# A decoder layer on one core: causal pooling by transposes and doubled sums in three groups, and a decay in two factors

## The chip, the core and the metric

The kernel runs on one core of a Trainium2 chip. The metric is the device time of one execution in microseconds. Before the change it is 1568.56 us, the median of 3 runs (1568.49 to 1571.36). The names used below: TensorE (PE) multiplies matrices, VectorE (DVE) and ScalarE (ACT) work element by element, GpSimd is POOL, and SP issues most of the transfers.

## The reference

One layer of a decoder on 256 tokens of 2048 channels, all in float32:

```
h = rmsnorm(x)
q, k, v, z, b, a, p, g_a, g_b = split(h @ w_in)
q, k, v = silu(causal_conv4(q, k, v));  q, k = l2norm(q), l2norm(k)
o   = gated_delta_rule(q, k, v, decay(a), sigmoid(b))   # 16 heads of 128, chunks of 64
y_a = rmsnorm(o) * silu(z)
y_b = (trailing_mean(p) - p) @ pool_w * pool_scale       # 4 groups of 512 channels
x  += (sigmoid(g_a) * y_a + sigmoid(g_b) * y_b) @ w_out
h = rmsnorm(x);  gate, up = split(h @ w_up)              # 2 x 5632
x  += (gelu(causal_conv3(gate)) * up) @ w_down
out = rmsnorm(x)
```

The trailing mean runs over the last 2, 4, 8 or 16 tokens, one window for each group of 512 channels; at the start of the sequence it divides by the tokens that there are. The delta rule is a recurrence over the tokens with a decay for each token and head: what token i gives to token j is weighted by the exponential of the sum of the log-decays between them.

## The kernel before

**Weights.** Nearly all of the work is products with weights. A weight matrix comes in tiles of 256 rows by 512 columns, 512 KB each, loaded over SP's queue (`load`, L124). ACT casts a tile to the matmul's format (L143, `whi`), and DVE subtracts that from the tile to get the part that the cast lost (L151, `wlo`). The input is split in the same way, and three matmuls (L181, L182, L183) give high times high, low times high and high times low. So `gemm_a` makes 12 matmuls of a weight tile. Four raw tiles and three pairs of split tiles are held, and `weights()` begins the tile two ahead of the one that it hands out (`AHEAD = 2`). The products of the MLP are made in the same way (L205 and L206, L1044 to L1046).

**Groups.** The mixing half runs over 4 groups, `g`, of 4 heads and 512 channels. In each, the products with weights come in the order K, Q, V, P (the pooled input), GB (the gate of the pooled branch), the pool product (the pooled input with `pool_w`, two tiles only, `nk = 4`), Z and GA. All but the pool product have 8 tiles. Between the matmuls runs the side work:

- Functions in the list `later` are run when the next product comes to its second tile. The convolutions of K and Q (`conv_silu`), the pooling (`pooled`) and the turning of the mixed result (`mixed`) come in this way.
- `side()` is called after every 6 matmuls. It takes one step of the generator `gdn`, the delta rule of the current group; a `yield` there is such a step, half a weight tile.

**Pooling.** `pooled` (L880 to L891) turns the evicted input `ev` and pools it in one go. It multiplies `ev` with a band matrix in float32 (L885, L887): the band holds one over the window, in the first tokens one over the count, less the identity, all times one half. The bands of the four windows are built once, by `fixed_parts` (L529 on), with memset, copies, `affine_select` and subtractions. ACT casts the result to `phi` (L890), and DVE subtracts to get `plo` (L891). The pool product reads both. The turning elsewhere is done by `turned`: 8 transposes (L226) into two PSUM tiles, `psg`, of which there are four buffers in all.

**The delta rule, `gdn`.** The 256 tokens lie in two halves of 128. Its steps, in order:

1. *Decay.* For two heads at a time DVE makes the triangular tiles r (L647, L648). Matmuls (L655, L656) sum the log-decays within each half, `pd0` and `pd1`; another (L658, with `onesr`, a tile of ones) sums those of the second half up to each of its tokens, `pdx`. ACT takes the exponentials (L659, L660), and for the pair of halves those of `pdx` with the first half's remaining sum, `tail`, as bias (L663). POOL clears the upper triangles (L665).
2. *Grams.* Matmuls of keys with keys and queries (L674, L676). DVE multiplies them with the norm factors and the decay to `ga0` (first half against both halves, L689) and `ga1` (second half, L693).
3. *Transfers.* The diagonal blocks of 32 go through memory, `cdd` (L707) and then `lb` (L710), so that one tile holds all blocks for the solve.
4. *Query norms.* A transpose on DVE, a reduction, the selection matmul (L725), and four small operations, `ro` (L729).
5. *Solve.* `LATE[g]` steps later, `tb` is set to the identity (L737), and 31 pairs of operations, `tmp` (L740) and `tb` (L742), three pairs a step, invert the blocks of 32. `tb` goes through memory (`tbd`, L747, then `TT`, L750) and is turned on DVE to `T` (L761).
6. *Merges.* Small matmuls join the blocks of 32 to 64 (from L782) and the blocks of 64 to 128 (to L811).
7. *Outputs.* `w1` (L817) solves the first half, `pr` (L822) carries it into the second, where `vt` takes it off (L823), `w2` (L827) solves the second half; `po[0]` and `po[1]` (L832 to L835) are the outputs of the halves. `po[1]` sums two products in PSUM, one with `ga0[384:512]` and `w1`, one with `ga1` and `w2`. Squares, norms, the gates (`gated`) and the turning follow.

**What sets the order.** The program is written as one stream. A scheduler orders each engine's instructions by its own model of time. Two places are ordered by hand: the start, and for the last group PE alone. There PE keeps the written order from the GA product on (`fixed_order`). In that group the delta rule waits before its merges (`while g == 3 and not ending`) until 6 tiles of GA are done; `step(n)` leaves n steps between the merges instead of one, and the first 6 tiles of two output products (`early`) cover what follows. The buffers of `mtile` (`m0` to `m7`) hold `phi` and `plo` of a group and later its mixed result; the other tiles have tags in the pool `mp`, and a tile with a tag in use waits for the one before it.

Of the kernel before, what the change touches and what calls it, by code (L numbers as in the profile page):

```python
# [13 lines left out]
P = 128  # L14
# [20 lines left out]
def kernel(  # L35
# [32 lines left out]
    def nm(s):  # L68
        cnt[0] += 1
        return f"{s}_{cnt[0]}"  # L70
# [376 lines left out]
    nc.vector.reciprocal(icnt, icnt)  # L447
    nc.vector.tensor_scalar(icnt, icnt, 0.5, None, op0=ALU.mult)
    idh = mp.tile([P, P], F32, name="idh")
# [19 lines left out]
    bat = mp.tile([64, 2, S], F32, tag="u", name="bat")  # L469
    nc.vector.tensor_copy(bat, pba[:64])  # L470
# [58 lines left out]
    def fixed_parts():  # L529
        for g, win in enumerate(WINDOWS):  # L530
            bd = bands[:, g, :]
            nc.gpsimd.memset(bd, 0.5 / win)
            nc.vector.tensor_copy(bd[:, 0:PAD], icnt[:, g, :])
            for cs in (slice(0, P + PAD), slice(P + PAD, NB)):
                b = bd[:, cs]
                n = cs.stop - cs.start
                nc.gpsimd.affine_select(b, b, pattern=[[1, n]], compare_op=ALU.is_ge, fill=0.0, base=0,
                                        channel_multiplier=-1)
                nc.gpsimd.affine_select(b, b, pattern=[[-1, n]], compare_op=ALU.is_ge, fill=0.0, base=win - 1,
                                        channel_multiplier=1)  # L540
                nc.vector.tensor_tensor(b[:, 0:P], b[:, 0:P], idh, op=ALU.subtract)
        nc.gpsimd.memset(Ta, 0.0)
        nc.gpsimd.memset(TTa, 0.0)
# [85 lines left out]
    def gdn(g, kq, vt, conv, res):  # L629
# [5 lines left out]
        sj = mp.tile([P, 2, 4], F32, tag="sj", name=nm("sj"))  # L635
        dec0 = mp.tile([P, 4, S], F32, tag="dec0", name=nm("dec0"))
        dec1 = mp.tile([P, 4, P], F32, tag="dec1", name=nm("dec1"))
        for hp in range(2):

            h0 = 2 * hp  # L640
            rx = []
            for part, gp in (("h", ghi.bitcast(F32)), ("l", glo)):
                r0 = mp.tile([P, 2, P], F32R, tag="r0" + part, name=nm("r0"))
                r1 = mp.tile([P, 2, P], F32R, tag="r1" + part, name=nm("r1"))
                for i in range(2):
                    hh = 4 * g + h0 + i
                    nc.vector.tensor_scalar(r0[:, i], tri, gp[:, 0, hh : hh + 1], None, op0=ALU.mult)  # L647
                    nc.vector.tensor_scalar(r1[:, i], tri, gp[:, 1, hh : hh + 1], None, op0=ALU.mult)  # L648
                rx.append((r0, r1))
            yield  # L650
            pd0 = pg([P, 2, P])
            pdx = pg([P, 2, P])
            pd1 = pg([P, 2, P])
            for n, (r0, r1) in enumerate(rx):
                mm(pd0, lowr, r0, start=(n == 0), stop=(n == 1))  # L655
                mm(pd1, lowr, r1, start=(n == 0), stop=(n == 1))  # L656
            for n, (r0, r1) in enumerate(rx):
                mm(pdx, onesr, r1, start=(n == 0), stop=(n == 1))  # L658
# [5 lines left out]
            for d in (dec0[:, h0 : h0 + 2, 0:P], dec1[:, h0 : h0 + 2, :]):  # L664
                nc.gpsimd.affine_select(d, d, pattern=[[0, 2], [1, P]], compare_op=ALU.is_ge, fill=0.0, base=0,  # L665
                                        channel_multiplier=-1)
            yield
        for hp in range(2):
# [18 lines left out]
            for h in (h0, h0 + 1):  # L687
                pg0, pg1 = grams[h - h0]
                nc.vector.scalar_tensor_tensor(ga0[:, h, :].rearrange("p (a s) -> p a s", a=2),  # L689
                                               pg0.rearrange("p (a s) -> p a s", a=2), sj[:, 0, h : h + 1],  # L690
                                               dec0[:, h, :].unsqueeze(1).to_broadcast([P, 2, S]),
                                               op0=ALU.mult, op1=ALU.mult)
                nc.vector.scalar_tensor_tensor(ga1[:, h, :].rearrange("p (a s) -> p a s", a=2),  # L693
                                               pg1, sj[:, 1, h : h + 1],
# [70 lines left out]
        while g == 3 and not ending:  # L765
            yield

        def step(n):
# [81 lines left out]
    for g in range(4):  # L850
# [24 lines left out]
        ps = gemm_a(xh, xl, KD)  # L875
        e = evict(ps)
        phi = mtile(g, [P, 4, S], F32R, nm("phi"))
        plo = mtile(4 + g, [P, 4, S], F32R, nm("plo"))

        def pooled(e=e, g=g, phi=phi, plo=plo):  # L880
            for f2 in range(2):
                pt = pg([P, 2, S])
                for ff in range(2):
                    fs = slice((2 * f2 + ff) * P, (2 * f2 + ff + 1) * P)
                    mm(pt[:, ff, P:S], e[:, 1, fs], bands[:, g, P + PAD : NB], start=True, stop=False,  # L885
                       skip_group_check=True)
                    mm(pt[:, ff, 0 : P + PAD], e[:, 0, fs], bands[:, g, 0 : P + PAD], start=False, stop=True,  # L887
                       skip_group_check=True)
                fs = slice(2 * f2, 2 * f2 + 2)
                nc.scalar.copy(phi[:, fs, :], pt)  # L890
                nc.vector.tensor_tensor(plo[:, fs, :], pt, phi[:, fs, :].bitcast(F32), op=ALU.subtract)  # L891

        later.append(pooled)

# [6 lines left out]
        tb = gate(gemm_a(xh, xl, KD), "th")  # L901
        ps = gemm_a(lambda k, t: phi[:, k, t * P : (t + 1) * P], lambda k, t: plo[:, k, t * P : (t + 1) * P], 4)
        yb = mp.tile([P, 2, 512], F32, tag="yb", name=nm("yb"))
# [227 lines left out]
```

## Time and profile before

| | before |
|---|---|
| median of 3 runs | 1568.56 us |
| the profiled execution | 1568.66 us |
| its span in the profile | 1566.9 us |
| mean granted clock of TensorE | 0.999 |
| weight loads issued by SP: w_in, w_up, w_down, w_out | 224, 176, 88, 32 of 512 KB |
| weight loads: pool_w | 8 of 512 KB |
| moved by all transfers | 304.23 MB, 194 GB/s in the mean |

The profile is of one execution. Its page gives the busy time of each engine and its share of the span, the chain of work that ended last, and groups of instructions. A group's line reads: source line, engine, operation, output and inputs, shape, number of instructions, then the busy time, the mean of one in nanoseconds, and the idle time before them with what ended it. A time line gives start and duration in microseconds from the start of the span, then the instruction, and in square brackets how long the engine stood idle before it and for what. A line of the list of waits reads: engine, output and line that waited, an arrow, what it waited for, then the time in all, the number of waits, and the longest. PE records overlap, since matmuls are pipelined: the distance from start to start is what a matmul costs in a row of them.

### The profile page before, as it was taken

To read this page: it belongs to the slowest core of one execution; us is meant where nothing else is said; L and a number is where in the kernel's file an instruction comes from. 1 tells how busy PE (TensorE), PEld (TensorE's weight loads), DVE (VectorE), ACT (ScalarE), POOL (GpSimd) and SP (SyncE) were. 2 spreads that over 40 slices of the span, in tenths; PEclk is the share of its full clock that TensorE was granted. 3 is DMA by queue.
4 is the path that set the end of the run, shared out by engine and by line. 5 is a ranking of instruction groups with operands and counts; after the bars stand their busy time and mean duration, and the time that the engine had idled before them with its cause. 6 is when DMAs were issued, how large, how long until landed. Compare 5 with 4: busy or idle time off the path is not lost.

```text
span 1566.9 us, 21271 instructions
## 1 busy us (share of the span) xinstructions
PE 1555.7 (99%) x8022; PEld 1307.4 (83%) x8022; DVE 1078.9 (69%) x1671; ACT 745.2 (48%) x956; POOL 43.3 (3%) x69
## 2 busy tenths in 40 slices
PE   9999999999999999999999999999999999999997
PEld 8878888888888888787888888888888888888886
DVE  6898749895698758796656666776666667444444
ACT  6545446354554546354544544444444444343443
POOL 2110001000010001000000000000000000000000
PEclk9999999999999999999999999999999999999999
DMA  8676657666676656665655555566556556656662
GB/s 272 199 229 199 195 161 220 196 201 178 181 220 196 198 162 193 212 204 169 216 185 177 189 189 188 188 190 189 188 186 191 189 187 213 199 191 210 202 224 89
DMA packets 168229, 304.23 MB, mean 194 GB/s; under 512 B 19234, under 2 KB 22834, under 8 KB 167998
## 3 DMA queue, kind: packets, MB, share of 16 engines
q1 hardware_dynamic: 165104, 297.84, 61.3%
q10 hardware_dynamic: 3022, 5.03, 0.9%
q8 instruction: 63, 1.03, 0.3%
q14 instruction: 40, 0.33, 0.1%
HBM read 297.56 MB, written 5.27 MB: 193 GB/s over the span
## 4 chain that ended last, share of the span: by engine, by line
PE 98%; DMA 1%; issue 1%; SPq 0%; ACT 0%; DVE 0%; POOLq 0%; POOL 0%
PE psm L183 15%; PE psm L181 15%; PE psm L182 15%; PE psm L205 10%; PE psg L205 10%; PE psg L206 5%; PE psm L206 5%; PE psg L1044 2%; PE psg L1046 2%; PE psg L1045 2%; PE psm L1045 2%; PE psm L1046 2%; PE psm L1044 2%; PE psm L312 1%; PE psg L674 1%; PE psg L226 1%
## 5 line engine op out<-in xcount | busy, mean ns | idle before, releaser
L151 DVE TENSOR_TENSOR wlo<-raw,whi 128x1024 fp32r<-128x1024 f32 x522 | 637.2, 1223 | 391.4 <-ACT whi L143 381.8
L143 ACT CAST whi<-raw 128x1024 fp32r<-128x1024 f32 x524 | 551.2, 1053 | 705.6 <-PE psm L182 313.0
L183 PE MATMUL psm<-wlo,xhl 128*128 128x512 f32 x864 | 339.7, 393 | 0.0
L181 PE MATMUL psm<-whi,xhl 128*128 128x512 f32 x864 | 338.9, 392 | 0.0
L182 PE MATMUL psm<-whi,xhl 128*128 128x512 f32 x864 | 338.5, 392 | 0.0
L205 PE MATMUL psm<-fhl,whi 128*128 128x512 f32 x704 | 246.2, 396 | 0.0
L205 PE MATMUL psg<-fhl,whi 128*128 128x512 f32 x704 | 238.0, 395 | 0.0
L206 PE MATMUL psm<-fhl,wlo 128*128 128x256 f32 x704 | 194.4, 279 | 0.0
L182 PEld LDWEIGHTS psm<-whi,xhl 128*128 128x128 f32 x864 | 162.2, 188 | 33.4
L183 PEld LDWEIGHTS psm<-wlo,xhl 128*128 128x128 f32 x864 | 162.3, 188 | 32.9 <-DVE wlo L151 0.2
L181 PEld LDWEIGHTS psm<-whi,xhl 128*128 128x128 f32 x864 | 162.3, 188 | 32.6
L206 PE MATMUL psg<-fhl,wlo 128*128 128x256 f32 x704 | 178.8, 279 | 0.0
L205 PEld LDWEIGHTS psm<-fhl,whi 128*128 128x128 f32 x704 | 131.4, 188 | 30.5
L205 PEld LDWEIGHTS psg<-fhl,whi 128*128 128x128 f32 x704 | 129.2, 188 | 24.2
L206 PEld LDWEIGHTS psg<-fhl,wlo 128*128 128x128 f32 x704 | 132.5, 188 | 6.9
L206 PEld LDWEIGHTS psm<-fhl,wlo 128*128 128x128 f32 x704 | 132.5, 188 | 1.1
L1044 PE MATMUL psg<-whi,hhi 128*128 128x512 f32 x168 | 65.5, 390 | 0.0
L1045 PE MATMUL psg<-whi,hlo 128*128 128x512 f32 x168 | 65.4, 389 | 0.0
L1044 PE MATMUL psm<-whi,hhi 128*128 128x512 f32 x168 | 65.4, 389 | 0.0
L1046 PE MATMUL psm<-wlo,hhi 128*128 128x512 f32 x168 | 65.4, 389 | 0.0
L1045 PE MATMUL psm<-whi,hlo 128*128 128x512 f32 x168 | 65.4, 389 | 0.0
L1046 PE MATMUL psg<-wlo,hhi 128*128 128x512 f32 x168 | 59.0, 389 | 0.0
(262 smaller groups left out, 1522.5 us busy)
## 6 DMA issues: line engine op xcount, KB each, us to landing
raw<-in_w_in_dram SPq DMA_DIRECT2D x224, 512.0 KB, 4.1
raw<-in_w_up_dram SPq DMA_DIRECT2D x176, 512.0 KB, 4.5
raw<-in_w_down_dram SPq DMA_DIRECT2D x88, 512.0 KB, 4.3
raw<-in_w_out_dram SPq DMA_DIRECT2D x32, 512.0 KB, 3.6
mv<-vrow SPq DMA_DIRECT2D x12, 512.0 KB, 5.6
taps<-in_conv_qkv_w_dram SPq DMA_DIRECT2D x16, 256.0 KB, 5.9
raw<-in_pool_w_dram SPq DMA_DIRECT2D x8, 512.0 KB, 5.9
vrow<-ev SPq DMA_DIRECT2D x4, 512.0 KB, 3.1
```

Of the source, the lines that this page charges most:

```text
L143: nc.scalar.copy(hi, raw)
L151: last_split[0] = nc.vector.tensor_tensor(lo, raw, hi.bitcast(F32), op=ALU.subtract).ins
L181: mm(ps[:, t, :], lh(k, t), hi[:, kk, :], start=(k == 0), stop=False)
L182: mm(ps[:, t, :], ll(k, t), hi[:, kk, :], start=False, stop=False)
L183: mm(ps[:, t, :], lh(k, t), lo[:, kk, :], start=False, stop=(k == nk - 1))
L205: mm(ps[f], hi[:, kk, fs], rhl(k), start=(k == 0), stop=False, skip_group_check=True)
L206: mm(ps[f][:, 1, :], lo[:, kk, fs], rhl(k)[:, 0, :], start=False, stop=(k == nk - 1), skip_group_check=True)
L226: nc.tensor.transpose(pt[:, ff, t * P : (t + 1) * P], src[:, t, f * P : (f + 1) * P], ident)
L312: mm(ps_k0[:, t, :], part(k, t), w[:, kk, :], start=(k == 0 and w is hi and part is xh), stop=(k == KD - 1 and w is lo))
L1044: mm(acc[c][t], lh(k, t), hi[:, kk, :], start=(k == 0), stop=False)
L1045: mm(acc[c][t], ll(k, t), hi[:, kk, :], start=False, stop=False)
L1046: mm(acc[c][t], lh(k, t), lo[:, kk, :], start=False, stop=(k == KF - 1))
```

## The change

**Pooling by turns and sums, groups 0 to 2.** `pooled` now transposes the evicted input (8 transposes by `turned`), and ACT copies the result from PSUM to `u`. DVE sums by doubling: each sum adds the tile to itself shifted by 1, 2, 4 tokens, so windows 2, 4 and 8 take one, two and three sums; ACT copies the first tokens, which have no partner. Then DVE multiplies the first `win` tokens by one over the count and subtracts `u`, and one operation over the rest multiplies by one over the window and subtracts `u`. ACT casts the whole to `phi`, DVE subtracts to `plo`, which is allocated only here, since its buffer holds a sum before. The input is evicted with half the norm factor, so the counts are not halved. Group 3 (window 16) keeps the band product under the name `banded`, and `bands` has one window instead of four.

**The decay across the halves as two factors.** The exponential of `pdx` plus `tail` is now a product: `tail` is the exponential of the first half's remaining sum, and `head` that of the second half's sum up to a token, both made once for all heads (`psh` is a new matmul). The matmuls of `pdx` and their exponentials go, and `dec0` has half its width. The part of `ga0` for the next half is scaled by `tail` alone, in an operation of its own. `head` comes in later: `vt` takes off `pr` times `head` in four operations, one a head, with `nhead` the negative; and the product of `ga0[384:512]` with `w1`, now `pa`, moves ahead of `w2`, is scaled by `head` on ACT into `vt[:, 0]`, and is added to `po[1]` on DVE.

**One step on.** In group 3 there is one more `yield` after the wait for `ending`, ahead of the first merge.

The tile `bat` takes the tag `w2` instead of `u`. In the diff a line of "..." leaves out the smaller parts: the factor one half of `icnt`, the names, the slices of `dec0` handed to `affine_select`.

```diff
-    onesr = mp.tile([P, P], F32R, name="onesr")
-    nc.vector.tensor_copy(onesr, ones)
...
-    nc.vector.tensor_copy(tail, psd)
...
+    nc.scalar.activation(tail, psd, AF.Exp)
+
+    psh = pg([P, NH])
+    mm(psh, tri, glog[:, 1, :], start=True, stop=True)
+    head = mp.tile([P, NH], F32, name="head")
+    nc.scalar.activation(head, psh, AF.Exp)
...
-    bands = mp.tile([P, 4, NB], F32, name="bands")
...
+    bands = mp.tile([P, NB], F32, name="bands")
...
-            for n, (r0, r1) in enumerate(rx):
-                mm(pdx, onesr, r1, start=(n == 0), stop=(n == 1))
-            nc.scalar.activation(dec0[:, h0 : h0 + 2, 0:P], pd0, AF.Exp)
+            nc.scalar.activation(dec0[:, h0 : h0 + 2, :], pd0, AF.Exp)
             nc.scalar.activation(dec1[:, h0 : h0 + 2, :], pd1, AF.Exp)
-            for i in range(2):
-                hh = 4 * g + h0 + i
-                nc.scalar.activation(dec0[:, h0 + i, P:S], pdx[:, i, :], AF.Exp, bias=tail[:, hh : hh + 1])
...
+                nc.vector.scalar_tensor_tensor(ga0h[:, :, own], pg0h[:, :, own], sj[:, 0, h : h + 1],
+                                               dec0[:, h, :].unsqueeze(1).to_broadcast([P, 2, P]),
                                                op0=ALU.mult, op1=ALU.mult)
+                nc.vector.tensor_scalar(ga0h[:, :, next_half], pg0h[:, :, next_half], sj[:, 0, h : h + 1],
+                                        tail[:, hh : hh + 1], op0=ALU.mult, op1=ALU.mult)
...
         while g == 3 and not ending:
+            yield
+        if g == 3:
             yield
...
-        nc.vector.tensor_tensor(vt[:, 1], vt[:, 1], pr, op=ALU.subtract)
+        for h in range(4):
+            nc.vector.scalar_tensor_tensor(vt[:, 1, h, :], pr[:, h, :], nhead[:, 4 * g + h : 4 * g + h + 1],
+                                           vt[:, 1, h, :], op0=ALU.mult, op1=ALU.add)
         yield from step(2)
+        pa = pg([P, 4, P])
+        for h in range(4):
+            mm(pa[:, h, :], ga0[:, h, 384:512], w1[:, h, :], start=True, stop=True)
+        for h in range(4):
+            nc.scalar.activation(vt[:, 0, h, :], pa[:, h, :], AF.Copy, scale=head[:, 4 * g + h : 4 * g + h + 1])
...
         for h in range(4):
-            mm(po[1][:, h, :], ga0[:, h, 384:512], w1[:, h, :], start=True, stop=False)
-            mm(po[1][:, h, :], ga1[:, h, P : 2 * P], w2[:, h, :], start=False, stop=True)
+            mm(po[1][:, h, :], ga1[:, h, P : 2 * P], w2[:, h, :], start=True, stop=True)
+        nc.vector.tensor_tensor(vt[:, 1], vt[:, 0], po[1], op=ALU.add)
+        po = [po[0], vt[:, 1]]
...
-        e = evict(ps)
+        e = evict(ps) if g == 3 else evict(ps, rsh)
...
+        def pooled(e=e, g=g, win=win, phi=phi, plo=plo):
...
+            u = mp.tile([P, 4, S], F32, tag="pu", name=nm("pu"))
+            for f2, pt in enumerate(turned(e)):
+                nc.scalar.copy(u[:, 2 * f2 : 2 * f2 + 2, :], pt)
+            src, n = u, 1
+            while n < win:
+                if n * 4 == win:
+                    dst = mp.tile([P, 4, S], F32, tag="pa", name=nm("pa"))
+                else:
+                    dst = mtile(4 + g, [P, 4, S], F32, nm("pb"))
+                nc.scalar.copy(dst[:, :, 0:n], src[:, :, 0:n])
+                nc.vector.tensor_tensor(dst[:, :, n:], src[:, :, n:], src[:, :, : S - n], op=ALU.add)
+                src, n = dst, 2 * n
+            pool = mp.tile([P, 4, S], F32, tag="pa", name=nm("pool"))
+            nc.vector.tensor_tensor(pool[:, :, 0:win], src[:, :, 0:win],
+                                    icnt[:, g, 0:win].unsqueeze(1).to_broadcast([P, 4, win]), op=ALU.mult)
+            nc.vector.tensor_tensor(pool[:, :, 0:win], pool[:, :, 0:win], u[:, :, 0:win], op=ALU.subtract)
+            nc.vector.scalar_tensor_tensor(pool[:, :, win:], src[:, :, win:], 1.0 / win, u[:, :, win:],
+                                           op0=ALU.mult, op1=ALU.subtract)
+            nc.scalar.copy(phi, pool)
+            plo.append(mtile(4 + g, [P, 4, S], F32R, nm("plo")))
+            nc.vector.tensor_tensor(plo[0], pool, phi.bitcast(F32), op=ALU.subtract)
+
+        later.append(banded if g == 3 else pooled)
```

More of the change, by code (lines that the diff above doesn't have):

```diff
@@ L468 @@
             mm(pba, hi[:, kk, :], xhl[:, k], start=(k == 0), stop=(k == KD - 1))
-    bat = mp.tile([64, 2, S], F32, tag="u", name="bat")
+    bat = mp.tile([64, 2, S], F32, tag="w2", name="bat")
     nc.vector.tensor_copy(bat, pba[:64])
@@ L529, in fixed_parts @@
     def fixed_parts():
[L530 to L541, printed above, removed]
+        win = WINDOWS[3]
+        nc.gpsimd.memset(bands, 0.5 / win)
+        nc.vector.tensor_scalar(bands[:, 0:PAD], icnt[:, 3, :], 0.5, None, op0=ALU.mult)
+        for cs in (slice(0, P + PAD), slice(P + PAD, NB)):
+            b = bands[:, cs]
+            n = cs.stop - cs.start
+            nc.gpsimd.affine_select(b, b, pattern=[[1, n]], compare_op=ALU.is_ge, fill=0.0, base=0,
+                                    channel_multiplier=-1)
+            nc.gpsimd.affine_select(b, b, pattern=[[-1, n]], compare_op=ALU.is_ge, fill=0.0, base=win - 1,
+                                    channel_multiplier=1)
+            nc.vector.tensor_tensor(b[:, 0:P], b[:, 0:P], idh, op=ALU.subtract)
         nc.gpsimd.memset(Ta, 0.0)
@@ L875, with banded @@
         ps = gemm_a(xh, xl, KD)
-        e = evict(ps)
+        e = evict(ps) if g == 3 else evict(ps, rsh)
         phi = mtile(g, [P, 4, S], F32R, nm("phi"))
-        plo = mtile(4 + g, [P, 4, S], F32R, nm("plo"))
-        def pooled(e=e, g=g, phi=phi, plo=plo):
+        plo = []
+        def banded(e=e, g=g, phi=phi, plo=plo):
+            plo.append(mtile(4 + g, [P, 4, S], F32R, nm("plo")))
             for f2 in range(2):
@@ L884, in pooled @@
                     fs = slice((2 * f2 + ff) * P, (2 * f2 + ff + 1) * P)
-                    mm(pt[:, ff, P:S], e[:, 1, fs], bands[:, g, P + PAD : NB], start=True, stop=False,
+                    mm(pt[:, ff, P:S], e[:, 1, fs], bands[:, P + PAD : NB], start=True, stop=False,
                        skip_group_check=True)
-                    mm(pt[:, ff, 0 : P + PAD], e[:, 0, fs], bands[:, g, 0 : P + PAD], start=False, stop=True,
+                    mm(pt[:, ff, 0 : P + PAD], e[:, 0, fs], bands[:, 0 : P + PAD], start=False, stop=True,
                        skip_group_check=True)
@@ L890, in pooled @@
                 nc.scalar.copy(phi[:, fs, :], pt)
-                nc.vector.tensor_tensor(plo[:, fs, :], pt, phi[:, fs, :].bitcast(F32), op=ALU.subtract)
-        later.append(pooled)
+                nc.vector.tensor_tensor(plo[0][:, fs, :], pt, phi[:, fs, :].bitcast(F32), op=ALU.subtract)
+        def pooled(e=e, g=g, win=win, phi=phi, plo=plo):
[18 more added lines that the diff above has]
+            nc.scalar.copy(phi, pool)
+            plo.append(mtile(4 + g, [P, 4, S], F32R, nm("plo")))
+            nc.vector.tensor_tensor(plo[0], pool, phi.bitcast(F32), op=ALU.subtract)
+        later.append(banded if g == 3 else pooled)
         def gate(ps, tag):
```

17 lines of the change are left out of this document (9 added, 8 removed).

## The prediction

> **What bounds the kernel now.** I read the page first, then the list of who waits for whom on TensorE, then time lines of single stretches, and last the order of instructions of both programs, engine by engine.
>
> ```profile
> span 1566.9 us, 21271 instructions
> PE 1555.7 (99%) x8022; PEld 1307.4 (83%) x8022; DVE 1078.9 (69%) x1671; ACT 745.2 (48%) x956; POOL 43.3 (3%) x69
> PE 98%; DMA 1%; issue 1%; SPq 0%; ACT 0%; DVE 0%; POOLq 0%; POOL 0%
> ```
>
> TensorE (PE) is busy for 99% of the span and makes up 98% of the chain that ended last. So a matmul taken away is time gained, a matmul added is time lost, and work on VectorE (DVE) or ScalarE (ACT) counts only where TensorE comes to wait for it. It hardly waits today:
>
> ```profile
> PE psg L782 <- DVE T L761: 1.5, 2, 0.8
> PE psm L242 <- POOL ones L232: 1.1, 1, 1.1
> PE psm L312 <- ACT whi L132: 0.6, 1, 0.6
> ```
>
> These are all its waits. The first, 1.5 us, is the first merge of the last group, where TensorE stands before L782; the other two are at the start. The profiled execution took 1568.66 us, 1.76 us around the span, and the median shown is 1568.56 us, so its sum may be read as one for the median.
>
> The weights set the pace. Twelve matmuls use one weight tile; ScalarE may cast a new tile only when TensorE has let go of the one three before it:
>
> ```profile
> L143 ACT CAST whi<-raw 128x1024 fp32r<-128x1024 f32 x524 | 551.2, 1053 | 705.6 <-PE psm L182 313.0 <-PE psm L205 127.8 <-PE psg L205 92.5
> 710.01 1.06 ACT L143 CAST whi<-raw 128x1024 fp32r<-128x1024 f32 x1 [1.67 <-PE psm L182]
> 712.73 1.05 ACT L143 CAST whi<-raw 128x1024 fp32r<-128x1024 f32 x1 [1.66 <-PE psm L182]
> ```
>
> The casts lie 2.72 us apart: that is a tile, 0.227 us a matmul. DVE's split (L151) follows each cast, so an operation that stands behind a split in DVE's queue cannot start before that tile's turn. I use this below.
>
> **Part 1, matmuls.** In three groups 8 fp32 band matmuls (two records each) give way to 8 transposes.
>
> ```profile
> 128.85 0.47 PE L885 MATMUL psg<-bands,ev 128*128 128x128 f32 x2
> ...
> 130.56 0.41 PE L887 MATMUL psg<-bands,ev 128*128 128x144 f32 x2
> 130.72 0.49 PE L183 MATMUL psm<-wlo,xhl 128*128 128x512 f32 x1
> ```
> ```profile
> 69.01 1.03 PE L226 MATMUL psg<-ident,ev 128*128 128x128 f32 x8
> 69.80 0.48 PE L182 MATMUL psm<-whi,xhl 128*128 128x512 f32 x1
> ```
> ```profile
> 78.83 0.40 PE L658 MATMUL psg<-r,onesr 128*128 128x256 f32 x2
> 79.06 0.39 PE L183 MATMUL psm<-wlo,xhl 128*128 128x512 f32 x1
> ```
>
> From first start to the next weight matmul the band product takes 130.72 - 128.85 = 1.87 us, eight transposes 69.80 - 69.01 = 0.79 us. Gain 1.08 us a group, 3.2 us in three. The 16 matmuls for the decay across the halves (L658) go; two take 0.23 us, so 1.8 us go. The products with ga0[384:512] are only moved. One small matmul of 16 columns comes (psh), at most the 0.23 us of that pair; I take 0.1. TensorE is rid of 4.9 us.
>
> The Trainium skill ("TensorE: Matmul & The Clock Gate", Part 4) gives about 275 ns for a 128x128 transpose within a kernel; at that price 24 would cost 6.6 us instead of 2.4 and this term would be 0.7 us. The rows above decide for 0.79 us per eight: they overlap.
>
> The smaller pieces I cost at nothing. The band tables of three groups, onesr and half the decay's exponentials go, from DVE, GpSimd and ACT, hidden behind matmuls. The product with the decay (L689) becomes two operations, and the vt update four; in the order these stand at least a tile ahead of the matmul that reads them. The last group's added sum has the 48 weight matmuls before its transposes as cover. If that cover were gone, each costs its own length, below 1 us.
>
> **Part 2, the pooled chain.** This is the price. Before, two casts and two subtractions from PSUM followed the band product. Now there are two copies, one to three sums, two edge operations, a combination, a cast of the whole tile and a subtraction, and TensorE's pool product (nk=4) needs cast and subtraction complete.
>
> ```profile
> L597 DVE TENSOR_TENSOR vt<-vt,mv 128x1024 f32<-128x1024 f32 x12 | 14.6, 1217 | 0.0
> L905 DVE SCALAR_TENSOR_TENSOR yb<-gate,yb 128x1024 f32<-128x1024 f32 x4 | 4.9, 1218 | 0.0
> L740 DVE TENSOR_TENSOR tmp<-lb,tb 128x248 f32<-128x248 f32 x4 | 1.7, 417 | 2.3 <-DMA lb<-cdd 2.3
> L737 DVE COPY tb<-idb 128x256 f32<-128x256 f32 x4 | 1.1, 286 | 0.0
> L843 DVE TENSOR_TENSOR ro<-ro,so 128x8 f32<-128x8 f32 x4 | 0.6, 155 | 0.0
> L890 ACT CAST phi<-psg 128x512 fp32r<-128x512 f32 x8 | 4.7, 586 | 4.2 <-PE psg L887 4.2
> ```
> ```profile
> 308.67 0.69 DVE L729 TENSOR_SCALAR ro<-psg 32x8 f32<-32x8 f32 x4 [1.23 <-PE psg L725]
> 309.39 1.22 DVE L151 TENSOR_TENSOR wlo<-raw,whi 128x1024 fp32r<-128x1024 f32 x1
> ```
>
> Count from the selection matmul (L725 now) that stands just ahead of the transposes in the new order. The pool product stands 34 weight matmuls behind them in groups 0 and 1 and 46 in group 2: TensorE arrives at 0.13 + 0.87 + 34 x 0.227 = 8.7 us, and at 11.4 us. The copies are done at 1.8 us; DVE has the four small ro operations until 1.0 and a split until 2.2 us.
>
> Group 1, in DVE's new order: sums to 3.4 and 4.6; a split to 5.7; copy of tb 6.0; edge and combination (0.16 + 1.22) 7.3; a tmp operation of the solve 7.7; edge 8.0; then the split of the pool weights' second tile to 9.15, a tb operation 9.5, subtraction 10.7 us. The cast (1.05) runs beside that, to 9.1. TensorE arrives at 8.7, does one matmul and goes on at 10.75: it loses 1.8 us. Group 2: sums 3.4, 4.6; split 5.7; tb 6.0; third sum 7.2; tmp 7.6; split 8.8; edge and combination 10.1; tb 10.5; edge 10.6; split 11.7; tmp 12.1; subtraction 13.3. It loses 13.3 - 11.4 - 0.2 = 1.7 us. Group 0, one sum and one split between: subtraction at 7.2, before 8.7, nothing lost. The terms have never run in this order, so I bound each of groups 1 and 2 by nothing (DVE ready early) and by 4 us (the solve's lb late, below), and take 1.8 and 1.7, the durations of rows.
>
> **Part 3, the first merge of the last group.** The added yield puts L782 half a tile later, 1.36 us. What it waits for:
>
> ```profile
> 711.10 1.22 DVE L151 TENSOR_TENSOR wlo<-raw,whi 128x1024 fp32r<-128x1024 f32 x1 [0.32 <-ACT whi L143]
> 712.24 0.17 DVE L742 TENSOR_TENSOR tb<-tb,tmp 128x8 f32<-128x8 f32 x1
> 713.82 1.23 DVE L151 TENSOR_TENSOR wlo<-raw,whi 128x1024 fp32r<-128x1024 f32 x1 [1.41 <-ACT whi L143]
> 719.99 1.84 DVE L761 STREAM_TRANSPOSE T<-TT 32x256 f32<-32x256 f32 x4 [2.23 <-DMA TT<-tbd]
> ```
> ```profile
> 712.76 1.85 SPq L747 DMA_DIRECT2D tbd<-tb  x4
> 717.31 1.81 SPq L750 DMA_DIRECT2D TT<-tbd  x4
> ```
> ```profile
> 719.33 0.39 PE L183 MATMUL psm<-wlo,xhl 128*128 128x512 f32 x1
> 720.48 0.24 PE L782 MATMUL psg<-T,ga 32*32 32x32 f32 x2 [0.77 <-DVE T L761]
> 721.41 0.69 PE L782 MATMUL psg<-T,ga 32*32 32x32 f32 x30 [0.69 <-DVE T L761]
> ```
>
> The solve's last operation (712.24) starts two transfers through memory, then T. TensorE could have gone on at 719.33 + 0.23 = 719.56 and had all at 721.41: today's loss is 1.8 us. In the new order that last operation no longer stands behind the split of 711.10 but behind the next one (713.82), with three more small operations ahead of it, and SP's queue has one more weight load before it. It ends near 715.05 + 4 x 0.2 = 715.8, and the transfers start about 3.1 us later than 712.76. T is there at 724.5, TensorE at 719.56 + 1.36 = 720.9: the loss becomes 3.6 us, 1.8 us more. Bounds: 1.4 us gained (the queue keeps its old pace) and 2.7 lost (a whole tile late, no relief).
>
> **Sum.** -4.9 + 1.8 + 1.7 + 1.8 = +0.4 us: 1568.66 + 0.4 = 1569.1 us. Gains and new waits cancel.
>
> **The rivals.**
> *The pooled chains are hidden* (20%): the sums lie in VectorE's idle time, as the 69% of the page would allow, and only the merge costs. Against it speaks the place of the splits in the queue. -4.9 + 1.8 = -3.1: 1565.6 us.
> *The change does all that it says* (13%): also the merge's wait shrinks by the 1.4 us of its step, because the solve's small operations run ahead. -4.9 - 1.4 = -6.3: 1562.4 us.
> *Slower: lb ahead in the queue* (18%). In groups 1 and 2 the tmp operation stands ahead of edge, split and subtraction, and waits for lb from memory.
>
> ```profile
> 306.15 1.73 SPq L710 DMA_DIRECT2D lb<-cdd  x4
> 311.85 0.42 DVE L740 TENSOR_TENSOR tmp<-lb,tb 128x248 f32<-128x248 f32 x1 [0.31 <-DMA lb<-cdd]
> ```
>
> lb takes 5.7 us from issue to use, and tmp already waited 0.31 us. With longer decay products ahead of it and one more weight load before it in SP's queue, I place lb at 7.1 to 7.9 us against tmp's turn at 7.3: it decides from there, microsecond for microsecond. One tile late, it costs 2 us more in each group: 1573.1 us.
> *Slower: the clock* (7%).
>
> ```profile
> 716.00:722.00 6.00, 4.55 (x49) 3.46 (x47) 3.10 (x6) 1.68 (x3) 0.00 (x0) 1.00 0.64 187
> 1550.00:1567.00 17.00, 8.83 (x39) 6.96 (x38) 7.79 (x16) 6.25 (x14) 1.10 (x2) 0.91 0.33 123
> ```
>
> The seventh number is the granted clock: 1.00 across today's wait, 0.91 at the end, where TensorE is idle for half of the stretch. A wait of 3.6 us lies between; if the clock then falls to half for as long, 3.6 us are worked off at half pace, 1.8 to 3.6 us more: about 1572 us. The Trainium skill ("TensorE: Matmul & The Clock Gate", Part 1) says that the gate closes to half after an idle window of about 3.4 us; the rows show no case in mid-kernel.
>
> **How the numbers follow.** The forecast has 42%; its own range is 1566 to 1571.5. Within 0.2% (3.1 us, about what a measurement can tell from no change) lie 1565.5 to 1571.8. Faster: the second rival's 13%, half of the first's, 2 of the forecast: 25%. Slower: 15 of lb's, the clock's 7, 2 of the forecast: 24%. Same: 51%. The range 1563.5 to 1573.0 leaves out about one in ten on each side.
>
> **What would show it.** Right: TensorE's list of waits names the pooled cast or subtraction for 3 to 4 us in two places, around the pool products of groups 1 and 2, none in group 0, and T for some 3 us. TensorE's busy time falls by 4 to 5 us. The first fails if no pool product waits, the third if T's wait is shorter than 1.5 us, the clock's if a stretch behind a wait shows less than 1.00. A wait elsewhere, at the grams, the selection matmul or a weight split, would make the forecast wrong.

## The result, and the profile after

The changed kernel takes 1575.63 us in the median of 11 runs (1570.72 to 1577.93). Before takes 1569.13 us (1568.41 to 1571.36, 11 runs). The ratio is 1.0035, with a 95% interval of 1.0027 to 1.0043. The forecast was 1569.1 us, no change, with a range that ended at 1573.0. It was wrong.

The profiled execution took 1570.72 us, and it is the fastest of the eleven. So this profile accounts for 2.1 us over the profiled execution of before (1568.66), and the other 5 us lie in runs that it doesn't show. First what it shows, in lines of the page:

```profile
span 1569.0 us, 21229 instructions
PE 1552.5 (99%) x7984; PEld 1303.8 (83%) x7984; DVE 1092.5 (70%) x1704; ACT 749.3 (48%) x967; POOL 47.2 (3%) x54
PE 96%; DMA 1%; DVE 1%; issue 1%; SPq 1%; ACT 0%; POOL 0%; POOLq 0%; DVEq 0%
```

TensorE has less to do, and its share of the chain has fallen from 98% to 96%. What took the place is in the list of its waits:

```profile
PE psg L786 <- DVE T L763: 2.8, 2, 2.1
PE psm L181 <- ACT phi L927: 2.4, 2, 1.5
PE psm L182 <- DVE plo L929: 2.0, 2, 1.0
```

The first line is the old wait for T, grown. The other two are new and stand at the pool products, two waits each, in groups 1 and 2. Group 0 has none. TensorE's time line shows the three places, each from the last matmul ahead of the wait:

```profile
312.59 0.39 PE L183 MATMUL psm<-wlo,xhl 128*128 128x512 f32 x1
314.44 0.49 PE L181 MATMUL psm<-whi,phi 128*128 128x512 f32 x1 [1.46 <-ACT phi L927]
315.96 0.50 PE L182 MATMUL psm<-whi,plo 128*128 128x512 f32 x1 [1.03 <-DVE plo L929]
...
493.67 0.39 PE L183 MATMUL psm<-wlo,xhl 128*128 128x512 f32 x1
495.04 0.50 PE L181 MATMUL psm<-whi,phi 128*128 128x512 f32 x1 [0.98 <-ACT phi L927]
496.55 0.50 PE L182 MATMUL psm<-whi,plo 128*128 128x512 f32 x1 [1.01 <-DVE plo L929]
...
721.41 0.39 PE L183 MATMUL psm<-wlo,xhl 128*128 128x512 f32 x1
723.91 0.24 PE L786 MATMUL psg<-T,ga 32*32 32x32 f32 x2 [2.11 <-DVE T L763]
724.84 0.69 PE L786 MATMUL psg<-T,ga 32*32 32x32 f32 x30 [0.69 <-DVE T L763]
```

A matmul takes 0.227 us in a row of them, so the time lost is start to start less 0.227 each. Group 1: 1.62 + 1.29 = 2.9 us. Group 2: 1.14 + 1.28 = 2.4 us. The merge: from 721.64 to 724.84, 3.2 us, where before lost 1.85. With the 4.9 us of matmuls that the prediction took off, that is -4.9 + 2.9 + 2.4 + 1.35 = +1.75 us, against 2.06 measured.

Why group 1 lost 2.9 and not 1.8 stands in VectorE's time line:

```profile
310.09 1.20 DVE L925 SCALAR_TENSOR_TENSOR pool<-pb,pu 128x1008 f32<-128x1008 f32 x1
312.81 0.42 DVE L742 TENSOR_TENSOR tmp<-lb,tb 128x248 f32<-128x248 f32 x1 [1.52 <-DMA lb<-cdd]
313.14 0.17 DVE L924 TENSOR_TENSOR pool<-pool,pu 128x16 f32<-128x16 f32 x1
313.23 1.22 DVE L151 TENSOR_TENSOR wlo<-raw,whi 128x1024 fp32r<-128x1024 f32 x1
314.69 1.22 DVE L929 TENSOR_TENSOR plo<-pool,phi 128x1024 fp32r<-128x1024 f32 x1
```

The pooled chain is done but for a 0.17 us edge, a split (L151) and the subtraction (L929), and stands still for 1.52 us, because the solve's first operation is ahead of the edge in VectorE's queue and waits for lb from memory. Group 2 has the same with 1.16 us.

For the other runs only the time, the span and the granted clock are known. Over the eleven, the clock goes from 0.998 (the profiled one) to 0.993, and the time goes with it. Span times clock is 1565 to 1568 us in all of them. The clock is given to 0.001, worth 1.6 us, so waits that differ by a microsecond or two could hide in this, but the greater part of the spread goes with the clock: 0.995 in the median run instead of 0.998 is worth some 4.7 us of the 4.9 between them. That is the lead for the experiments.

### The profile page after: what moved, and what is told of

Same layout as the page of the kernel before. It is cut to its first block, busy times and chain, and to the rows that moved or that the text cites. A ratio compares the mean times of both kernels' runs of the same rounds, so it can differ in the third digit from the quotient of the medians.

```text
span 1569.0 us, 21229 instructions
## 1 busy us (share of the span) xinstructions
PE 1552.5 (99%) x7984; PEld 1303.8 (83%) x7984; DVE 1092.5 (70%) x1704; ACT 749.3 (48%) x967; POOL 47.2 (3%) x54
## 4 chain that ended last, share of the span: by engine, by line
PE 96%; DMA 1%; DVE 1%; issue 1%; SPq 1%; ACT 0%; POOL 0%; POOLq 0%; DVEq 0%
PE psm L182 14%; PE psm L181 14%; PE psm L183 14%; PE psm L205 10%; PE psg L205 10%; PE psg L206 5%; PE psm L206 5%; PE psg L1082 2%; PE psg L1083 2%; PE psg L1084 2%; PE psm L1082 2%; PE psm L1084 2%; PE psm L1083 2%; PE psm L312 1%; PE psg L671 1%
## 5 line engine op out<-in xcount | busy, mean ns | idle before, releaser
L151 DVE TENSOR_TENSOR wlo<-raw,whi 128x1024 fp32r<-128x1024 f32 x522 | 636.9, 1222 | 371.9 <-ACT whi L143 369.1
```

Source lines behind the costliest of these rows:

```text
L151: last_split[0] = nc.vector.tensor_tensor(lo, raw, hi.bitcast(F32), op=ALU.subtract).ins
```

## The experiments

Theory A says that the place of an operation in VectorE's queue makes the waits, and that behind a long wait TensorE's clock falls in most runs. Its rivals say that the waits themselves vary, or that the clock has to do with the other engines' work. Time in us, medians; each kernel ran beside before on the same chip.

| | median (range, runs) | before beside it | ratio, 95% interval | clock |
|---|---|---|---|---|
| e1 changed kernel again | 1573.83 (1571.63 to 1575.68, 11) | 1570.42 | 1.0024 (1.0015 to 1.0033) | 0.995 to 0.997 |
| e2 pooling alone | 1572.02 (1570.84 to 1573.82, 11) | 1570.42 | 1.0012 (1.0004 to 1.0021) | 0.996 to 0.998 |
| e3 two factors alone | 1565.21 (1564.88 to 1565.64, 5) | 1570.42 | 0.9965 (0.9952 to 0.9977) | 0.998 to 0.999 |
| e4 added step alone | 1567.32 (1566.48 to 1568.16, 11) | 1570.42 | 0.9978 (0.9970 to 0.9987) | 0.998 to 0.999 |
| e5 group 2's solve later | 1568.56 (1566.70 to 1569.44, 11) | 1569.90 | 0.9987 (0.9979 to 0.9996) | 0.997 to 0.998 |
| e6 merge a tile earlier | 1574.12 (1572.19 to 1575.95, 11) | 1569.90 | 1.0027 (1.0019 to 1.0036) | 0.996 to 0.998 |
| e7 bands in group 2 too | 1569.99 (1567.53 to 1571.27, 11) | 1569.90 | 0.9998 (0.9989 to 1.0007) | 0.996 to 0.998 |
| e8 e7, group 1's solve later | 1565.02 (1564.80 to 1566.99, 7) | 1569.90 | 0.9973 (0.9963 to 0.9984) | 0.998 to 0.999 |
| e9 e6 with the wait filled | 1571.65 (1571.10 to 1573.81, 11) | 1569.17 | 1.0014 (1.0005 to 1.0023) | 0.997 to 0.999 |
| e10 e3 again | 1565.52 (1564.80 to 1566.64, 11) | 1569.17 | 0.9977 (0.9969 to 0.9986) | 0.998 to 0.999 |
| e11 e8 again | 1565.13 (1564.70 to 1566.30, 8) | 1569.17 | 0.9975 (0.9965 to 0.9985) | 0.998 to 0.999 |

**e1, the changed kernel again**, nothing edited.

> The changed kernel once more, nothing edited. Theory A, the clock: its eleven runs lie between 1570.72 and 1577.93 us with granted clocks of 0.998 to 0.993, and span times clock is 1565 to 1568 us in every one, so the profiled execution is the one run without a loss of clock, and the typical one loses 4 to 5 us more to a lower clock behind the long waits of TensorE. Then the median is 1574 to 1576 us, and if the profile is of a typical run, the granted clock is below 1.00 in the 4 to 8 us behind a pool product of group 1 or 2 (near 314 and 495 us) or behind the first merge of the last group (near 725 us). Theory B, the waits themselves are longer in typical runs, since the pooled chain or lb comes late by chance: then the waits at those three places are longer than 2.9, 2.5 and 3.2 us, at a clock of 1.00.

Its profiled execution took 1573.59 us. TensorE at the merge (start, duration), and then the stretches behind it, where the number after the engines is the granted clock:

```profile
722.29 0.39 PE L183 MATMUL psm<-wlo,xhl 128*128 128x512 f32 x1
725.23 0.24 PE L786 MATMUL psg<-T,ga 32*32 32x32 f32 x2 [2.54 <-DVE T L763]
726.16 0.69 PE L786 MATMUL psg<-T,ga 32*32 32x32 f32 x30 [0.69 <-DVE T L763]
...
728.03 0.63 PE L182 MATMUL psm<-whi,xhl 128*128 128x512 f32 x1
728.46 0.63 PE L183 MATMUL psm<-wlo,xhl 128*128 128x512 f32 x1
```

```profile
727.00:728.00 1.00, 1.00 (x4) 0.78 (x4) 0.83 (x1) 0.68 (x3) 0.00 (x0) 0.77 0.17 66
728.00:729.00 1.00, 1.00 (x4) 0.78 (x3) 0.00 (x0) 0.00 (x0) 0.00 (x0) 0.50 0.20 14
729.00:730.00 1.00, 1.00 (x4) 0.81 (x3) 0.00 (x0) 0.00 (x0) 0.00 (x0) 0.50 0.70 168
730.00:731.00 1.00, 1.00 (x4) 0.74 (x4) 0.00 (x0) 0.00 (x0) 0.00 (x0) 0.53 0.84 287
```

Weight matmuls start 0.43 us apart instead of 0.227, at a clock of one half. The loss is 0.23 + 0.5 + 0.5 + 0.47 = 1.7 us, that is, 3.4 us at half pace. In the first profile the wait at this place, 3.2 us instead of 3.6, passed without it. Part of theory B holds too: the waits at the pool products are 3.1 and 3.15 us here, 0.9 us longer in all than in the first profile, and the merge's is 0.4 us longer. With the 1.7 us of clock that makes 3.0 us, against 2.87 between the two profiled executions. So the clock is the greater part, and longer waits are the rest. Three places at 1.7 us each above the first profile would give 1570.7 + 5.1 = 1575.8 us, near the first median of 1575.6; but no profile shows more than one place that pays, so this sum is not shown.

The Trainium skill ("TensorE: Matmul & The Clock Gate", Part 1) says that a free-running window of some 3.4 us decides the clock, and that it halves after a window of idling. The length agrees with this run, 3.4 us. But no idle time of that length was needed here: TensorE's longest standstill ahead of the drop was 2.7 us (722.52 to 725.23), and in the 3.4 us ahead of it, 724.1 to 727.5, it did 32 small and three full matmuls.

**e2, pooling alone.** Before, with the new `pooled`, its eviction and its one band table, the rest as it was.

```diff
...
-        later.append(pooled)
+        later.append(banded if g == 3 else pooled)
```

> Before with the pooling by transposes and sums in groups 0 to 2 alone; the decay in one factor and the merge as before. By the sum: 3.2 us less matmul work. In DVE's order the subtraction of group 1 stands one weight split later still than in the changed kernel (behind the split of the tile two after the pool product's first), so TensorE should lose 3.5 to 4.5 us there; in group 2 the subtraction stands two splits earlier than in the changed kernel, so 0 to 1 us; the merge as before. Profile without a loss of clock: 1568.7 - 3.2 + 4 + 0.5 = 1570 us. Theory A (clock falls behind long waits): median 1 to 5 us above that, 1571 to 1575, with a spread of several us. Theory B: median within 1 us of the lowest run. If pooling is not the cause at all, the time is below 1566.

```profile
PE psm L181 <- ACT phi L913: 3.3, 1, 3.3
```

```profile
317.00:318.00 1.00, 0.88 (x3) 0.68 (x4) 1.00 (x3) 0.07 (x1) 0.00 (x0) 0.67 0.34 131
318.00:319.00 1.00, 1.00 (x4) 0.81 (x3) 0.97 (x3) 0.00 (x0) 0.00 (x0) 0.50 0.81 139
```

One wait in group 1, none in group 2, as the order said, and the half clock behind it, at a pool product this time. TensorE lost 3.5 us there (313.66 to 317.12), so by its waits alone this execution would be at 1569.0 us, and 1.7 us of half clock make it 1570.7. It took 1571.91: 1.2 us of it are not accounted for. The median of the runs is 3 us above the sum without clock.

**e3, the two factors alone.** Before, with the edits of the decay and nothing else.

```diff
-            for n, (r0, r1) in enumerate(rx):
-                mm(pdx, onesr, r1, start=(n == 0), stop=(n == 1))
...
+        nc.vector.tensor_tensor(vt[:, 1], vt[:, 0], po[1], op=ALU.add)
+        po = [po[0], vt[:, 1]]
```

> Before with the decay in two factors alone, bands in all four groups, no added step. By the sum: 1.7 us less matmul work. In DVE's order the last operation of the last group's solve stands one weight split earlier than before, so the 1.8 us wait at the first merge should shrink to 0 to 0.5 us. 1568.7 - 1.7 - 1.5 = 1565.5 us, at a clock of 0.999, and no spread beyond that of before. The rival, that the decay's extra operations make lb late and so the solve: a time of 1567 to 1569 and the merge's wait as before or longer.

1565.21 us, and no wait at the first merge is left in its list. VectorE's time line shows the solve's last operation:

```profile
709.19 0.18 DVE L746 TENSOR_TENSOR tb<-tb,tmp 128x8 f32<-128x8 f32 x1
709.92 1.23 DVE L151 TENSOR_TENSOR wlo<-raw,whi 128x1024 fp32r<-128x1024 f32 x1 [0.55 <-ACT whi L143]
```

It ends ahead of the split at 709.92, which answers to the one at 711.10 in before; there it stood behind it. The clock stays at 0.998 to 0.999, and the runs lie within 0.8 us.

**e4, the added step alone.**

```diff
         while g == 3 and not ending:
             yield
+        if g == 3:
+            yield
```

> Before with the one added step ahead of the first merge of the last group, nothing else. DVE's order is that of before, so T is ready at the same time, and TensorE has half a weight tile, 1.36 us, more to do ahead of it: the wait of 1.8 us shrinks to 0.5, the time to 1567.3 us. The rival: the step shifts the later merges onto each other or takes cover from the end of the group, and the time stays at 1568.6 or rises.

1567.32 us, and here too the wait is gone from the list. Both e3 and e4 lie further below the before beside them (5.2 and 3.1 us) than matmuls and wait account for (3.55 and 1.85). Before's own runs beside e1 to e4 reach from 1568.3 to 1571.6 us, at clocks of 0.997 to 0.999. So before seems to pay some clock as well. Of its 80 runs behind this table, 32 lie below 1569.3 us, with a mean clock of 0.9986, and 36 above 1570.2, with 0.9978. They are 2.2 us apart, and the clock is worth 1.2 us of that. No profile of before caught a slower run, so whether its wait was longer than 1.85 us there isn't known.

**e5, group 2's solve later.**

```diff
-LATE = (26, 24, 22, 18)
+LATE = (26, 24, 26, 18)
```

> The changed kernel with one number changed: in group 2 the solve is called four steps later (LATE 26 for 22). In DVE's new order the operations of the solve that wait for lb stand behind the pooled chain of group 2 instead of within it, and the last operation of the last group's solve stands one weight split earlier (230 instead of 231). Theory (place in DVE's queue, lb included): the wait at group 2's pool product shrinks from 2.5 to about 0.5 us, that at the last group's first merge from 3.2 to 0.5 us, that of group 1 stays at 2.9. Sum without a loss of clock: 1568.7 - 4.9 + 2.9 + 0.5 + 0.5 - 1.85 = 1565.8 us; with some loss of clock behind group 1's wait a median up to 1567.5. Rival (the chain is too long by itself, lb is no matter): group 2's wait stays above 2 us, and the time at 1568 or more.

```profile
PE psm L181 <- ACT phi L927: 2.3, 1, 2.3
PE psm L182 <- DVE plo L929: 1.6, 2, 1.0
...
PE psg L786 <- DVE T L763: 0.6, 1, 0.6
```

Group 2's wait is now 0.6 us (the second of the two on plo), and that for T is 0.6 us. One number moved two waits, since both hang on places in VectorE's queue. Group 1's wait did not stay at 2.9 us. It is 2.4 + 1.3 = 3.7 us (from 312.39 on, where TensorE is done), though the edit doesn't touch group 1: the first operation of its solve waits 2.32 us for lb here, where it waited 1.52 in the first profile and 1.67 in e1. So lb's arrival differs from one execution to the next. The median is 2.8 us above the sum. In the profiled run (1568.68 us) 0.8 of that is the longer wait, and behind it half clock for 3.4 us costs some 1.6.

**e6, the merge a tile earlier.** Before, with the wait made longer and nothing added to do.

```diff
-            ps = gemm_a(xh, xl, KD, range(6))
+            ps = gemm_a(xh, xl, KD, range(5))
             ending.append(True)
-            ps = gemm_a(xh, xl, KD, range(6, 8), ps)
+            ps = gemm_a(xh, xl, KD, range(5, 8), ps)
```

> Before with the first merge of the last group one weight tile earlier on TensorE (the merges may begin after 5 tiles of GA instead of 6), everything else as before. T is ready when it was, so TensorE waits 1.85 + 2.72 = 4.6 us instead of 1.85, and without a loss of clock the time is 2.7 us above the clean time of before: 1568.5 + 2.7 = 1571.2 us. Theory A (the clock falls behind a long wait, and the more surely the longer it is): the granted clock drops to about half behind the merge in most runs, the median is 1573 to 1575 us at a mean clock of 0.995 to 0.997. Rival (the loss of clock of the changed kernel belongs to the pool products or to VectorE's added work): 1571 us with the clock and spread of before.

```profile
716.99 0.39 PE L183 MATMUL psm<-wlo,xhl 128*128 128x512 f32 x1
720.61 0.31 PE L782 MATMUL psg<-T,ga 32*32 32x32 f32 x2 [3.23 <-DVE T L761]
721.54 1.06 PE L782 MATMUL psg<-T,ga 32*32 32x32 f32 x30 [0.62 <-DVE T L761]
```

```profile
720.00:721.00 1.00, 0.31 (x2) 0.17 (x2) 0.85 (x2) 0.00 (x0) 0.00 (x0) 0.68 0.44 81
...
727.00:728.00 1.00, 1.00 (x6) 0.83 (x4) 0.36 (x1) 0.00 (x0) 0.00 (x0) 0.91 0.00 0
```

A wait of 4.3 us, and half clock from about 720.4 to 727.2: 6.8 us, twice 3.4, of which TensorE still waited for the first 1.2. The median is 1574.12 us, 2.9 above the 1571.2 that the wait costs by its length. No pooling and no other decay is in this kernel, so the loss belongs to TensorE's wait and not to the work that the change adds.

**e7, bands in group 2 too.** The changed kernel, with the transposes and sums in groups 0 and 1 only. The copy u lies in another buffer for want of room.

```diff
+BANDED = (2, 3)
...
-        later.append(banded if g == 3 else pooled)
+        later.append(banded if g in BANDED else pooled)
...
-            u = mp.tile([P, 4, S], F32, tag="pu", name=nm("pu"))
+            u = mtile(5 + g, [P, 4, S], F32, nm("pu"))
```

> The changed kernel with the band product left in group 2 as well as in group 3: transposes and sums in groups 0 and 1 only (the copy u sits in a buffer of a later group, to make room). In DVE's order the last solve's last operation stands at split 229, two earlier than in the changed kernel. So what moves the last group's solve is the pooled chain of group 2, and here the wait at the first merge is gone, group 1's pool product waits 2.9 us as in the changed kernel, group 2's does not. Sum: 1568.7 - 1.85 - 1.7 - 2.2 + 2.9 = 1565.9 us. If a wait of 2.9 us in two pieces at the pool product costs clock as well, the median is 1 to 2 us above that with a spread of 2 us or more; if only the merge costs clock, the runs lie within 1 us of 1565.9.

Its lines are numbered one higher. The wait for T is gone, so it was group 2's pooled chain that pushed the last group's solve back. Group 1 was longer and costlier than I wrote. VectorE, TensorE, and the clock:

```profile
312.94 0.42 DVE L745 TENSOR_TENSOR tmp<-lb,tb 128x248 f32<-128x248 f32 x1 [2.34 <-DMA lb<-cdd]
```

```profile
311.90 0.39 PE L184 MATMUL psm<-wlo,xhl 128*128 128x512 f32 x1
314.58 0.50 PE L182 MATMUL psm<-whi,phi 128*128 128x512 f32 x1 [2.29 <-ACT phi L930]
316.10 0.79 PE L183 MATMUL psm<-whi,plo 128*128 128x512 f32 x1 [1.02 <-DVE plo L932]
```

```profile
315.00:317.00 2.00, 0.98 (x3) 0.81 (x3) 2.00 (x3) 1.63 (x3) 0.00 (x0) 0.50 0.58 146
...
321.00:323.00 2.00, 2.00 (x9) 1.59 (x8) 1.11 (x1) 0.85 (x1) 0.00 (x0) 0.81 0.00 0
```

lb lands at 312.9, as in the changed kernel (312.8), while TensorE is there 0.7 us sooner (312.13, against 312.82). So the wait is 3.7 us, as in e5, and half clock lasts two stretches, to 321.8. A wait that I had not in the theory came too: at 676.38 TensorE stood 0.9 us for a weight split (L152).

**e8, group 1's solve later.** To e7 comes:

```diff
-LATE = (26, 24, 22, 18)
+LATE = (26, 26, 22, 18)
```

> As the one before, and group 1's solve is called two steps later (LATE 26 for 24), so that in DVE's order its operations, lb's wait among them, stand behind the pooled chain of group 1. Theory (place in the queue, lb included): group 1's wait shrinks from 2.9 to about 0.8 us, since the subtraction is then done at 313.8 where TensorE is there at 312.8; no other wait. Sum: 1568.7 - 1.85 - 1.7 - 2.2 + 0.8 = 1563.8 us, with the spread of a kernel that hardly waits (within 1 us). Rival (lb is no matter): 1565.9 as the one before. This is also the version meant to beat both kernels.

```profile
311.09 0.17 DVE L927 TENSOR_TENSOR pool<-pool,pu 128x16 f32<-128x16 f32 x1
311.24 1.22 DVE L152 TENSOR_TENSOR wlo<-raw,whi 128x1024 fp32r<-128x1024 f32 x1
...
312.58 1.22 DVE L932 TENSOR_TENSOR plo<-pool,phi 128x1024 fp32r<-128x1024 f32 x1
```

The operation that waits for lb no longer stands between them; of the solve, only the copy of tb (0.28 us, at 312.38) is still ahead of the subtraction. The subtraction ends at 313.8 as worked out, TensorE waits 0.6 us in the list, and the clock is 0.998 to 0.999. Counted from the small ro operations ahead of the chain, the subtraction ends 3.0 us sooner than in e7, and 2.34 of that is e7's wait for lb. From e7, one number took 5 us off the median.

**e9, the wait filled.** e6, with 14 matmuls in the wait whose result nobody reads.

```diff
+        if g == 3:
+            pf = pg([P, 2, S])
+            for _ in range(14):
+                mm(pf, lowr, xhl[:, 0], start=True, stop=True)
```

> The kernel with the 4.6 us wait at the last group's first merge (before, merges one tile earlier), and in that wait 14 matmuls on TensorE whose result nobody reads (14 x 0.227 = 3.2 us, ending about 0.2 us before T comes). Nothing else moves; T is ready when it was. Theory A (the clock falls because TensorE stands idle): TensorE now idles under 1.5 us in all, so the clock stays at 0.998 to 0.999, and the time is that of the wait alone, 1571.2 us with a spread of 1 us, 3 us less than the same kernel without them (1574.1) although it does 3.2 us more of matmuls. Rival (the loss of clock has to do with the other engines or with the lateness itself, not with TensorE being idle): 1574 us and 0.996 as without them, or more, since work was added.

```profile
717.51 3.33 PE L770 MATMUL psg<-xhl,lowr 128*128 128x512 f32 x14
720.77 0.24 PE L786 MATMUL psg<-T,ga 32*32 32x32 f32 x2
721.68 0.69 PE L786 MATMUL psg<-T,ga 32*32 32x32 f32 x30 [0.67 <-DVE T L761]
```

```profile
722.00:723.00 1.00, 1.00 (x25) 0.87 (x20) 0.10 (x1) 0.77 (x4) 0.00 (x0) 1.00 0.81 311
```

More work for TensorE, and less time: 1571.65 us, at a mean clock of 0.998. That is 2.5 us less than e6, or 1.7 if each is counted from the before beside it (1569.17 and 1569.90). The two profiled executions, 1571.65 and 1574.12, show where it comes from. T comes when it came (720.26, against 720.12), and no stretch around the merge is below 1.00. From the 30 small matmuls to the start of the 18th weight matmul behind them e9 takes 4.6 us, where e6 takes 7.1. So only TensorE's idling has changed, and with it the clock. For this wait that settles the cause.

**e10 and e11, the two best beside each other.** e3 and e8 once more.

> The two factors of the decay alone, once more, beside the next kernel on one chip: 1565.2 us and a clock of 0.998 or 0.999, as measured.

> Transposes and sums in groups 0 and 1, two factors, the added step, group 1's solve two steps later, once more. By the sum it should lie 2.2 - 0.85 = 1.3 us below the two factors alone (1563.9); measured on another run of the chip it was 1565.0 against 1565.2. Theory: the sum holds when both run on one chip, 1 to 1.5 us apart. Rival: the 0.85 us wait costs clock in some runs, and the two are the same within 0.5 us.

1565.52 and 1565.13 us. The rival's number holds: 0.4 us apart, and the ranges overlap. Its reason, clock lost behind the 0.85 us wait, isn't shown: both kernels have 0.998 to 0.999 in all runs. By the profiled spans they are 0.7 us apart (1563.8 and 1563.1). Either beats before by about 4 us and the changed kernel by 8 to 10. That transposes and sums in groups 0 and 1 are worth anything beside the two factors isn't shown.

## Why the prediction was wrong, point by point

- **Part 1, matmuls.** The mechanism is right. From the first of eight transposes to the next weight matmul it is 0.83 us in the changed kernel (304.15 to 304.98), where I had 0.79. The busy time fell by 3.2 us only, not by the 4 to 5 that I named as the sign. The busy sum also holds the full length of each matmul that stands alone, and there are more of these now; that this is the whole difference isn't shown.
- **Part 2, the pooled chain.** The places were right: groups 1 and 2, not group 0. So was TensorE's arrival, 8.8 us behind the selection matmul against 8.7. The sizes, 1.8 and 1.7 us, came out at 2.9 and 2.4. The difference is lb, which I had as a rival of its own and left out of the forecast. I had put it at 7.1 to 7.9 us against its turn at 7.3; in group 1 it came 1.5 us after its turn, at 8.8, and in e5 and e7 at 9.6. e5 and e8 show that it was lb's place in the queue.
- **Part 3, the first merge.** 1.35 us more, where I had 1.8. The solve ended at 716.5 (I had 715.8), behind one more split, as I wrote:

```profile
714.54 1.22 DVE L151 TENSOR_TENSOR wlo<-raw,whi 128x1024 fp32r<-128x1024 f32 x1 [0.26 <-ACT whi L143]
...
716.31 0.18 DVE L744 TENSOR_TENSOR tb<-tb,tmp 128x8 f32<-128x8 f32 x1
```

  T was there at 724.84 (I had 724.5), TensorE at 721.64 (I had 720.9). e7 adds what put the solve there: group 2's pooled chain.
- **The sum.** +0.4 us, against +2.06 for the profiled execution. That alone would have been in the range.
- **The step that failed** is the one on the clock, which the sum put at nothing. I gave it 7%, for one place, and only for a wait of 3.6 us, since no row of before showed a loss in mid-kernel. The sum took every wait at its length. In the profiled executions half clock stands behind each wait of 3.5 us and more: 3.5 in e2, 3.6 at e1's merge, 3.7 in e5 and e7, 4.3 in e6. It stands behind none of 3.2 us or less: the changed kernel's 2.9, 2.4 and 3.2, e1's 3.1 and 3.15 at the pool products. Each time it cost between 1.6 and some 2.8 us, so my price for one place, 1.8 to 3.6 us, was about right. I had it as an exception at one place out of three, with pool waits of 1.8 and 1.7 us, which e1's profile shows at 3.1 and 3.15 and e5's at 3.7 in group 1. The median is made of runs with a lower clock, 0.995 against 0.998, and the first profile was of one that kept it. How the median's loss is shared among the three places stays open.
- **What I left unasked.** Before's three times reached from 1568.49 to 1571.36, with a profile at the low end. A spread of 3 us in a kernel whose only wait in mid-run is 1.85 us was a hint that a wait has a price beyond its length.

## What to carry to other kernels

Where TensorE is the bound, a new wait costs its own length and, once it reaches some 3.5 us as in five profiled executions here, 3.4 us or more at half clock behind it. So trading 1 us of matmuls for a wait of 2 us loses by the length already, and again in each run in which the wait comes out longer. Price it at both, and look at the spread of several runs, not at one profile. And when a chain gets longer on an engine, look at what stands within it in that engine's queue: here an operation that waited for a transfer did the harm, and calling it two steps later took the harm away.

## What the runs showed of the hardware

- Half clock came in stretches of 3.4 us (e1, e2, e5), each 1.6 to 1.7 us of loss, or of 6.8 us (e6, e7), about 2.5 to 2.8 us of loss, since TensorE still waited for the first 1.1 to 1.2 us.
- Which wait pays: in the profiles, all of 3.5 us and more and none of 3.2 us and less. Whether the length alone decides it or chance as well isn't shown, since no profile has a wait between 3.2 and 3.5 us, or two waits of one length with different ends. The length itself differs from run to run: 2.9, 3.1 and 3.7 us at group 1's pool product in three executions whose group 1 is the same.
- The idle time needn't be in one piece: in e7 the clock fell at 315.0, 0.4 us after the first matmul behind a standstill of 2.45 us, and the longest standstill ahead of e1's drop was 2.7 us.
- Matmuls that do nothing keep the clock up: e9 does 3.2 us more of them than e6 and its profiled execution is 2.5 us shorter.
